# Products on quarter and half tiles of TensorE: an order tied product to product, and an order tied to its place only

## The chip, the cores and the metric

The kernel runs on one core of a Trainium2 chip. Its metric is the device time of one execution in microseconds (us); lower is better. Engines are named as in the profile: PE (TensorE matmul), PEld (its weight load), DVE (VectorE), ACT (ScalarE), POOL (GpSimd) and SP (SyncE, which issues most of the loads).

## What is computed

The reference is a two-layer encoder on 256 tokens of width 1024. Each layer runs two token mixers side by side, a gated DeltaNet in both directions and a differential attention. The change touches one step of the DeltaNet: the inverse of a unit triangular matrix for every chunk, head and direction, cut here to its lines.

```python
L = jnp.where(strict, jnp.einsum('bhncd,bhnmd->bhncm', kb, k) * decay, 0.0)
T = lax.linalg.triangular_solve(eye + L, jnp.broadcast_to(eye, L.shape),
                                left_side=True, lower=True, unit_diagonal=True)
u = jnp.einsum('bhncm,bhnme->bhnce', T, vb)
```

The kernel works with chunks of 128 tokens, two per sequence. There are 8 heads, in two groups of four, and two directions, so 32 triangles of 128 x 128 in each layer.

## The kernel before, in words

A layer is a row of projections (weights streamed from HBM, 512 columns at a time) with the DeltaNet's and the attention's small work laid between them. A projection (`proj_tm`) takes each weight block as two parts, `hi` (a cast on ACT, line 308) and `lo` (raw minus hi on DVE, line 310), and makes three products of 128 x 512 on PE for every block and token half (lines 324 to 326). In this document such a product is called a wide one. The tiles are `pp_gb`, `pp_ga` and `pp_pb` for the two merge gates and the attention's output projection.

The triangles are inverted in steps. 32 x 32 diagonal blocks are inverted by substitution on DVE. `merges(g)`, for head group g, then joins pairs of them to 64 x 64: it makes `y64p` (line 926), copies it on ACT, and makes the products `zt64` (line 939, 32 of them) and `z64` (line 944, 16 of them), each of 32 x 32. Each of these products lives on one of the sixteen 32 x 32 places of the PE array, given by the partitions it reads and those it writes. ACT then writes them, negated, back into the triangle `U_` (line 951) and into `T64` (line 954). `join()` does the same from 64 to 128 for both groups at once, on the four 64 x 64 places: `y128p` and `zt128`, each 32 products made by `quarters` (line 967), with copies on ACT behind each (lines 974, 976 and 984). From then on `chunks(g)` uses the finished triangle: `y1p`, `sp`, `ks`, `y2p`, `qs`, `po`, full products of 128 x 128 (lines 998 and 1037). `gram`, called by `weigh_q`, makes the products `kq` (line 789), also 128 x 128 and for four heads at a time, whose result DVE multiplies into `B` (line 830). A product in full f32 leaves two records in the trace.

The order is made by a scheduler when the kernel is built; each engine then runs its list strictly in that order, waiting by semaphores. `behind(x)` forbids the scheduler to issue what stands under it before instruction x has been issued; it adds no wait. `run(gen, at)` sets `mark["pin"]` to a certain wide product, the place of a step, and gives the step a high priority. Before the change, the first product of `zt64` is behind the pin, and each further one is behind the product before it; `quarters` chains its products in the same way.

On the other engines, this stretch also has: DVE's gating of the attention output (`ob`, line 1203), its transposition (`zb`, line 249) for a trip through DRAM issued by POOL, and its split (`ybT`, lines 263 and 265); DVE's `ktm` scaling (line 1010); and `key_sums`, which transposes `kq` on DVE (`tb_q`, line 135), squares it on ACT (line 1052), sums it on DVE into `qss` (line 1053), sends that through DRAM, and reduces it on DVE to `ssq` (line 1059).

Of the kernel before, what the change touches and what calls it, by code (L numbers as in the profile page):

```python
# [49 lines left out]
def hybrid_encoder(  # L50
# [19 lines left out]
    V, S, G, T = nc.vector, nc.scalar, nc.gpsimd, nc.tensor  # L70
# [24 lines left out]
    def bank_c(name):  # L95
        return ps_c.tile([P, 512], F32, tag="c", name=name)
# [7 lines left out]
    mark = {}  # L104
# [23 lines left out]
    blk = lambda b: slice(32 * b, 32 * b + 32)  # L128
# [141 lines left out]
    def behind(ins):  # L270
        return nullcontext() if ins is None else tc.issue_after(ins)
# [122 lines left out]
    halves = (slice(0, 64), slice(64, P))  # L394
# [6 lines left out]
    def srcdst(d, mm):  # L401
        return (2 * mm, 2 * mm + 1) if d == 0 else (2 * mm + 1, 2 * mm)
# [6 lines left out]
    for _ in range(5):  # L409
        mm = T.matmul(idle[:, :P], ones, ones, start=True, stop=True)  # L410
# [23 lines left out]
    for m in range(NM):  # L434
        mm = T.matmul(pos_p[:, m : m + 1], pos_r[:, m * P : (m + 1) * P], ones[0:1, 0:1], start=True, stop=True)
# [71 lines left out]
    for l in range(DEPTH):  # L507
# [120 lines left out]
        for kt in range(KT):  # L628
            for part in range(2):
                T.matmul(abp[0:64, :SEQ], wabr[:, kt, :], hT[kt // 4][:, part, kt % 4, :],  # L630
                         start=kt == 0 and part == 0, stop=kt == KT - 1 and part == 1)
# [3 lines left out]
        for m in range(NM):  # L635
            T.matmul(abq[:, m * 32 : (m + 1) * 32], abT[:, m * P : (m + 1) * P], id2,
                     start=True, stop=True)
# [244 lines left out]
        tix = lambda d, c, j4: (2 * d + c) * 4 + j4  # L882
        flat = lambda ap: ap.rearrange("p b e -> p (b e)")
        every = [(c, j4) for c in range(NM) for j4 in range(4)]
# [14 lines left out]
        def merges(g):  # L899

            U = U_[:, g]
            T64 = work.tile([P, 16, 64], F32, tag="w4c", name=f"T64{l}{g}", bufs=4)
            parts[g] = U, T64
            G.memset(T64[blk(0), 0:8, 32:64], 0.0)
            G.memset(T64[blk(3), 8:16, 0:32], 0.0)
            for b in range(4):
                co = 32 * (b % 2)
                (nc.sync if g else G).dma_start(out=T64[blk(b), :, co : co + 32],
                                                in_=udr[1, b, g].rearrange("t j i -> j t i"))
            yield  # L910
            for b in range(4 if g == 0 else 0):
                G.dma_start(out=U_[blk(b), :, :, blk(b)].rearrange("j g t i -> j (g t) i"),
                                  in_=udr[0, b].rearrange("g t j i -> j (g t) i"))
            yield
            v4 = lambda ap: ap.rearrange("p (c h i) -> p c h i", c=NM, h=4)
            y64p = v4(bank_c(f"y64p{l}{g}")[:, :256])
            y64 = work.tile([P, NM, 4, 32], F32, tag="w2c", name=f"y64{l}{g}", bufs=3)

            order = [(c, j4, mm, d) for c, j4 in every for mm in range(2) for d in range(2)]
            order.sort(key=lambda k: k != (0, 0, 1, 1))  # L920
            first = mark["pin"]
            for n_, (c, j4, mm, d) in enumerate(order):
                b0, b1 = srcdst(d, mm)
                co = 32 * (b0 % 2)
                with behind(first):
                    mm_ = T.matmul(y64p[blk(b1), c, j4, :], A[blk(b0), g, c, j4, blk(b1)],
                                   T64[blk(b0), tix(d, c, j4), co : co + 32], start=True, stop=True)
                if n_ == 0:
                    first = mm_.ins
            S.copy(y64, y64p)  # L930
            yield
            first = mark["pin"]
            zt64 = v4(bank_c(f"zt64{l}{g}")[:, :256])
            z64 = v4(bank_c(f"z64{l}{g}")[:, :256])
            for c, j4 in every:
                for mm, d in ((0, 0), (1, 1), (1, 0), (0, 1)):
                    b0, b1 = srcdst(d, mm)
                    with behind(first):
                        first = T.matmul(zt64[blk(b0), c, j4, :], y64[blk(b1), c, j4, :],
                                         U[blk(b1), tix(d, c, j4), blk(b1)], start=True, stop=True).ins  # L940
                for d in range(2):
                    b0, b1 = srcdst(d, d)
                    with behind(first):
                        first = T.matmul(z64[blk(b1), c, j4, :], U[blk(b1), tix(d, c, j4), blk(b1)],
                                         y64[blk(b1), c, j4, :], start=True, stop=True).ins
            for d in range(2):
                td = slice(8 * d, 8 * d + 8)
                fl = lambda z, b: z[blk(b)].rearrange("p c h i -> p (c h) i")
                for mm in range(2):
                    b0, b1 = srcdst(d, mm)  # L950
                    S.mul(U[blk(b0), td, blk(b1)], fl(zt64, b0), -1.0)
                b0, b1 = srcdst(d, d)
                co = 32 * (b0 % 2)
                S.mul(T64[blk(b1), td, co : co + 32], fl(z64, b1), -1.0)
            yield

        def join():

            v4 = lambda ap: ap.rearrange("p (c h i) -> p c h i", c=NM, h=4)
            every4 = [(c, j4, g, d) for c, j4 in every for g in range(2) for d in range(2)]  # L960

            def quarters(ps, lhs, rhs, row):
                last_ = mark["pin"]
                for c, j4, g, d in every4:
                    rows = halves[row(d)]
                    with behind(last_):
                        last_ = T.matmul(ps[g][halves[1 - row(d) if g == 0 else row(d)], c, j4, :],
                                         lhs(g, d, c, j4), rhs(g, d, c, j4), start=True, stop=True).ins

            y128p = [v4(bank_c(f"y128p{l}{g}")) for g in range(2)]  # L970
            y128 = [work.tile([P, NM, 4, 64], F32, tag="w2c", name=f"y128{l}{g}", bufs=3) for g in range(2)]
            quarters(y128p, lambda g, d, c, j4: A[halves[d], g, c, j4, halves[1 - d]],
                     lambda g, d, c, j4: parts[g][1][halves[d], tix(d, c, j4), :], lambda d: d)
            S.copy(y128[0], y128p[0])
            for d in range(2):
                S.copy(y128[1][halves[1 - d]], y128p[1][halves[d]])
            yield
            zt128 = [v4(bank_c(f"zt128{l}{g}")) for g in range(2)]
            quarters(zt128, lambda g, d, c, j4: y128[g][halves[1 - d], c, j4, :],
                     lambda g, d, c, j4: parts[g][0][halves[1 - d], tix(d, c, j4), halves[1 - d]], lambda d: 1 - d)  # L980
            for g in range(2):
                for d in range(2):
                    ha, hb = halves[d], halves[1 - d]
                    S.mul(parts[g][0][ha, 8 * d : 8 * d + 8, hb],
                          zt128[g][hb if g else ha].rearrange("p c h i -> p (c h) i"), -1.0)
            yield
# [204 lines left out]
        with tc.high_priority(offset=HP):  # L1191
            spread_blocks()
        mg = [merges(0), merges(1)]
        step(mg)
        step(mg)
# [201 lines left out]
```

## Time and profile before

| | |
|---|---|
| median of 3 runs | 749.97 us (749.54 to 751.45) |
| the profiled execution's own time | 749.41 us |
| its span (first to last instruction) | 747.6 us |
| granted clock of TensorE | 0.997 |
| PE busy | 738.6 us |
| DVE busy | 587.1 us |
| ACT busy | 482.5 us |
| POOL busy | 139.5 us |

In the timeline, a row has the start in us from the span's start, the time covered, the engine, the source line, the operation, what it writes and reads, and how many records were merged; at the end, in brackets, idle time ahead of it and what ended it. Since PE pipelines its products, its rows overlap, and the distance from one start to the next tells what a product costs. In the waits, a row has who waited for whom, the total, the number of times and the longest.

The region of the change lies at about 245 to 300 us in the first layer and 610 to 665 us in the second.

### The profile page before, as it was taken

How to read it: one execution, taken by the hardware profiler on the slowest of the kernel's cores; microseconds unless marked ns; L12 is line 12 of the kernel's file. 1: busy time of each engine (PE TensorE's matmuls, PEld its weight loads, DVE VectorE, ACT ScalarE, POOL GpSimd, SP SyncE). 2: the span in 40 equal slices, each digit the busy share in tenths (PEclk: the TensorE clock that was granted, in tenths of full speed). 3: DMA queues.
4: the chain of work that ended last, by engine and by line, in shares of the span. 5: the costliest groups of instructions: out<-in, count | busy, mean ns of one | idle time of the engine just before them, and what ended most of it. 6: DMA issues, size and time to landing. Idle time of an engine off the chain costs nothing.

```text
span 747.6 us, 13920 instructions
## 1 busy us (share of the span) xinstructions
PE 738.6 (99%) x5176; PEld 638.2 (85%) x5176; DVE 587.1 (79%) x1109; ACT 482.5 (65%) x1024; POOL 139.5 (19%) x221
## 2 busy tenths in 40 slices
PE   9999999999999999999999999999999999999996
PEld 6999889987888889988889899889778887988885
DVE  8696898999985975578677779999999679447782
ACT  6657875667876585645456578565687757766552
POOL 6004110112022422100000150202110424301000
PEclk9999999999999999999999999999999999999998
DMA  8755567776667462567674466767666747435641
GB/s 262 237 170 169 170 176 196 211 210 197 209 182 178 135 201 83 171 207 240 201 232 137 128 191 187 217 172 229 195 174 192 198 139 217 130 102 187 219 141 57
DMA packets 73734, 135.46 MB, mean 181 GB/s; under 512 B 12944, under 2 KB 13921, under 8 KB 73666
## 3 DMA queue, kind: packets, MB, share of 16 engines
q1 hardware_dynamic: 64750, 113.65, 50.8%
q0 software_dynamic: 7936, 19.35, 8.9%
q10 hardware_dynamic: 980, 1.58, 0.6%
q8 instruction: 41, 0.67, 0.4%
q14 instruction: 27, 0.22, 0.1%
HBM read 125.53 MB, written 9.01 MB: 180 GB/s over the span
## 4 chain that ended last, share of the span: by engine, by line
PE 90%; DVE 3%; issue 2%; ACT 2%; DMA 2%; POOL 1%; POOLq 0%; DVEq 0%; ACTq 0%
PE pp_vb L369 4%; PE pp_qk L325 4%; PE pp_qk L326 3%; PE pp_qk L324 3%; PE sc L1073 2%; PE pp_o L369 2%; PE pf_k L385 2%; PE pp_za L325 2%; PE pf_v L385 2%; PE pf_v L389 2%; PE pp_zb L324 2%; PE pf_q L387 2%; PE pf_k L387 2%; PE pf_k L389 2%; PE pf_q L385 2%
## 5 line engine op out<-in xcount | busy, mean ns | idle before, releaser
L325 PE MATMUL pp_qk<-lo_qk,hT 128*128 128x512 f32 x128 | 50.5, 395 | 0.3 <-DVE lo_qk L310 0.2
L326 PE MATMUL pp_qk<-hi_qk,hT 128*128 128x512 f32 x128 | 49.9, 390 | 0.0
L310 DVE TENSOR_TENSOR lo_qk<-raw_qk,hi_qk 128x1024 fp32r<-128x1024 f32 x32 | 39.1, 1221 | 10.3 <-ACT hi_qk L308 10.0
L324 PE MATMUL pp_qk<-hi_qk,hT 128*128 128x512 f32 x128 | 45.1, 393 | 0.0
L308 ACT CAST hi_qk<-raw_qk 128x1024 fp32r<-128x1024 f32 x28 | 29.4, 1049 | 23.5 <-PE pp_qk L326 12.4
L1083 ACT ACTIVATE es<-sc,mx 128x256 f32<-128x256 f32 x64 | 29.6, 474 | 19.5 <-DVE mx L1081 19.5
L387 PE MATMUL pf_q<-hT,hi_q 128*128 128x256 f32 x128 | 36.1, 286 | 0.0
L385 PE MATMUL pf_k<-hT,hi_k 128*128 128x256 f32 x128 | 36.0, 287 | 0.0
L385 PE MATMUL pf_v<-hT,hi_v 128*128 128x256 f32 x128 | 35.8, 285 | 0.0
L387 PE MATMUL pf_v<-hT,hi_v 128*128 128x256 f32 x128 | 35.8, 284 | 0.0
L385 PE MATMUL pf_q<-hT,hi_q 128*128 128x256 f32 x128 | 35.7, 284 | 0.0
L387 PE MATMUL pf_k<-hT,hi_k 128*128 128x256 f32 x128 | 35.7, 283 | 0.0
L389 PE MATMUL pf_q<-hT,lo_q 128*128 128x256 f32 x128 | 35.2, 288 | 0.0
L389 PE MATMUL pf_v<-hT,lo_v 128*128 128x256 f32 x128 | 34.5, 287 | 0.0
L310 DVE TENSOR_TENSOR lo_pb<-raw_pb,hi_pb 128x1024 fp32r<-128x1024 f32 x16 | 19.5, 1221 | 18.9 <-ACT hi_pb L308 18.8
L389 PE MATMUL pf_k<-hT,lo_k 128*128 128x256 f32 x128 | 34.3, 283 | 0.0
L308 ACT CAST hi_pa<-raw_pa 128x1024 fp32r<-128x1024 f32 x16 | 16.8, 1052 | 22.3 <-PE pp_pa L326 16.1
L679 DVE SCALAR_TENSOR_TENSOR cvq<-pf_q,cw,cvq 128x254 f32<-128x254 f32 (+1 forms) x64 | 30.0, 479 | 0.9 <-ACT cvq L675 0.2
L679 DVE SCALAR_TENSOR_TENSOR cvk<-pf_k,cw,cvk 128x254 f32<-128x254 f32 (+1 forms) x64 | 29.0, 477 | 1.3 <-ACT cvk L675 0.6
L679 DVE SCALAR_TENSOR_TENSOR cvv<-pf_v,cw,cvv 128x254 f32<-128x254 f32 (+1 forms) x64 | 29.7, 475 | 0.1
L325 PEld LDWEIGHTS pp_qk<-lo_qk,hT 128*128 128x128 f32 x128 | 24.0, 188 | 6.7 <-DVE lo_qk L310 1.7
L310 DVE TENSOR_TENSOR lo_pa<-raw_pa,hi_pa 128x1024 fp32r<-128x1024 f32 x16 | 19.6, 1224 | 11.1 <-ACT hi_pa L308 11.1
(415 smaller groups left out, 2543.0 us busy)
## 6 DMA issues: line engine op xcount, KB each, us to landing
raw_qk<-in_w_in_dram SPq DMA_DIRECT2D x32, 512.0 KB, 3.8
raw_k<-in_w_in_dram SPq DMA_DIRECT2D x16, 512.0 KB, 4.5
raw_q<-in_w_in_dram SPq DMA_DIRECT2D x16, 512.0 KB, 3.7
raw_v<-in_w_in_dram SPq DMA_DIRECT2D x16, 512.0 KB, 3.9
raw_zb<-in_w_in_dram SPq DMA_DIRECT2D x16, 512.0 KB, 3.8
raw_za<-in_w_in_dram SPq DMA_DIRECT2D x16, 512.0 KB, 3.8
raw_ga<-in_w_in_dram SPq DMA_DIRECT2D x16, 512.0 KB, 4.6
raw_pb<-in_w_pb_dram SPq DMA_DIRECT2D x16, 512.0 KB, 3.9
```

The costliest lines, as they stand in the source:

```text
L308: high = (V.tensor_copy if kp in turned else S.copy)(hi[:, :, :n], raw[:, :, :n]).ins
L310: mark[nm, kp] = high, V.tensor_tensor(lo[:, :, :n], raw[:, :, :n], hi[:, :, :n].bitcast(F32), ALU.subtract).ins
L324: T.matmul(o, act[kt // 4][:, 0, kt % 4, ts_], hi, start=kt == 0, stop=False)
L325: T.matmul(o, act[kt // 4][:, 0, kt % 4, ts_], lo, start=False, stop=False)
L326: mark["proj"] = T.matmul(o, act[kt // 4][:, 1, kt % 4, ts_], hi, start=False, stop=kt == KT - 1).ins
L369: mark["proj"] = T.matmul(o, act[kt // 4][:, pa, kt % 4, ts_], ws[kt][1 + pw], start=kt == 0 and n_ == 0, stop=kt == KT - 1 and n_ == 2).ins
L385: T.matmul(o, hi[:, cs], act[kt // 4][:, 0, kt % 4, :], start=first, stop=False, skip_group_check=True)
L387: T.matmul(o, hi[:, cs], act[kt // 4][:, 1, kt % 4, :], start=False, stop=False, skip_group_check=True)
L389: T.matmul(o, lo[:, cs], act[kt // 4][:, 0, kt % 4, :], start=False, stop=done, skip_group_check=True)
L679: V.scalar_tensor_tensor(ca[:, o0:o1], acc[:, b, o0 + sft : o1 + sft], cw[:, j, cb : cb + 1], ca[:, o0:o1], ALU.mult, ALU.add)
L1073: mm = T.matmul(sp[n][:, qt * SEQ : (qt + 1) * SEQ], qkT[h // 4][rows, 0, h % 4, qt * P : (qt + 1) * P], qkT[h // 4][rows, 1, h % 4, :], s ...
L1083: S.activation(es[:, n, qt, :], spv[:, qt, :], AF.Exp, bias=mx[:, n, qt : qt + 1], accum_out=s_all[:, h, n, qt : qt + 1])
```

## The change

Three things change in the source. In `merges`, all 32 products of `zt64` now come first and the 16 of `z64` after them, where before four of the one and two of the other alternated. The products of `zt64` are each behind the step's pin only, no longer behind one another, and those of `z64` have no tie. In `quarters`, each product is behind the pin only. No operation is added or removed, and no tile, buffer or semaphore is written by hand.

```diff
             for c, j4 in every:
-                for mm, d in ((0, 0), (1, 1), (1, 0), (0, 1)):
-                    b0, b1 = srcdst(d, mm)
-                    with behind(first):
-                        first = T.matmul(zt64[blk(b0), c, j4, :], y64[blk(b1), c, j4, :],
-                                         U[blk(b1), tix(d, c, j4), blk(b1)], start=True, stop=True).ins
+                for mm in range(2):
+                    for d in range(2):
+                        b0, b1 = srcdst(d, mm)
+                        with behind(first):
+                            T.matmul(zt64[blk(b0), c, j4, :], y64[blk(b1), c, j4, :],
+                                     U[blk(b1), tix(d, c, j4), blk(b1)], start=True, stop=True)
+            for c, j4 in every:
                 for d in range(2):
                     b0, b1 = srcdst(d, d)
-                    with behind(first):
-                        first = T.matmul(z64[blk(b1), c, j4, :], U[blk(b1), tix(d, c, j4), blk(b1)],
-                                         y64[blk(b1), c, j4, :], start=True, stop=True).ins
+                    T.matmul(z64[blk(b1), c, j4, :], U[blk(b1), tix(d, c, j4), blk(b1)],
+                             y64[blk(b1), c, j4, :], start=True, stop=True)
...
             def quarters(ps, lhs, rhs, row):
-                last_ = mark["pin"]
                 for c, j4, g, d in every4:
-                    rows = halves[row(d)]
-                    with behind(last_):
-                        last_ = T.matmul(ps[g][halves[1 - row(d) if g == 0 else row(d)], c, j4, :],
-                                         lhs(g, d, c, j4), rhs(g, d, c, j4), start=True, stop=True).ins
+                    with behind(mark["pin"]):
+                        T.matmul(ps[g][halves[1 - row(d) if g == 0 else row(d)], c, j4, :],
+                                         lhs(g, d, c, j4), rhs(g, d, c, j4), start=True, stop=True)
```

The scheduler then makes another order. It is shown at three places of layer 0; layer 1 has the same moves. The numbers in the names tell tiles apart: `zt_3358` and `z_3359` are `zt64` and `z64` of head group 1, `zt_3453` and `zt_3454` are `zt128` of groups 0 and 1, and `B_371<-kq_2855` is DVE's use of the last `kq`.

PE where the gate `pp_gb` ends and `pp_ga` begins, before:

```order
L789 MATMUL kq_2855<-kq_359 128x128
L939 MATMUL zt_3358<-U__96,y_3268 32x32
L789 MATMUL kq_2855<-kq_359 128x128
L939 MATMUL zt_3358<-U__96,y_3268 32x32
L789 MATMUL kq_2855<-kq_359 128x128
L939 MATMUL zt_3358<-U__96,y_3268 32x32
L789 MATMUL kq_2855<-kq_359 128x128
L939 MATMUL zt_3358<-U__96,y_3268 32x32
L944 MATMUL z_3359<-y_3268,U__96 32x32 x2
```

The same place now:

```order
L940 MATMUL zt_3358<-U__96,y_3268 32x32 x32
L945 MATMUL z_3359<-y_3268,U__96 32x32 x16
L325 MATMUL pp_gb_2765<-lo_gb_2820,hT_1_127 128x512
L326 MATMUL pp_gb_2765<-hi_gb_2819,hT_1_127 128x512
L324 MATMUL pp_gb_2766<-hi_gb_2819,hT_1_127 128x512
L325 MATMUL pp_gb_2766<-lo_gb_2820,hT_1_127 128x512
L326 MATMUL pp_gb_2766<-hi_gb_2819,hT_1_127 128x512
L789 MATMUL kq_2855<-kq_359 128x128 x4
```

The 48 small products of group 1 are in one piece, five wide products ahead of `kq`, and no `kq` product stands among them.

PE at `zt128`, in the gate `pp_ga`, before:

```order
L967 MATMUL zt_3453<-U__96,y_3416 64x64 x2
L324 MATMUL pp_ga_2897<-hi_ga_2952,hT_1_127 128x512
L325 MATMUL pp_ga_2897<-lo_ga_2953,hT_1_127 128x512
L967 MATMUL zt_3454<-U__96,y_3417 64x64 x2
L967 MATMUL zt_3453<-U__96,y_3416 64x64 x2
```

The same place now:

```order
L326 MATMUL pp_ga_2897<-hi_ga_2916,hT_0_126 128x512
L966 MATMUL zt_3453<-U__96,y_3416 64x64 x8
L966 MATMUL zt_3454<-U__96,y_3417 64x64 x8
L966 MATMUL zt_3453<-U__96,y_3416 64x64 x2
L966 MATMUL zt_3454<-U__96,y_3417 64x64 x2
```

The 32 products of `zt128` are in one piece, and stand about one and a half weight blocks earlier in the gate than before (ahead of `hi_ga_2934`, not within `hi_ga_2952`).

DVE in the same stretch, from the gating of the first token half on, before:

```order
L1203 SCALAR_TENSOR_TENSOR ob_1_384<-ob_1_384,rb_2865,zb_1_386 128x128 x4
L310 TENSOR_TENSOR lo_ga_2917<-raw_ga_2918,hi_ga_2916 128x1024
L1010 TENSOR_TENSOR ktm_360<-ktm_360,kds_372 128x512
L830 TENSOR_TENSOR B_371<-kq_2855,B_371 128x1024
L1010 TENSOR_TENSOR ktm_360<-ktm_360,kds_372 128x512
L1203 SCALAR_TENSOR_TENSOR ob_1_384<-ob_1_384,rb_2865,zb_1_386 128x128 x4
L249 STREAM_TRANSPOSE zb_1_386<-ob_1_384 128x4x4x32
L310 TENSOR_TENSOR lo_ga_2935<-raw_ga_2936,hi_ga_2934 128x1024
```

The same place now:

```order
L1202 SCALAR_TENSOR_TENSOR ob_1_384<-ob_1_384,rb_2865,zb_1_386 128x128 x4
L249 STREAM_TRANSPOSE zb_1_386<-ob_1_384 128x4x4x32
L830 TENSOR_TENSOR B_371<-kq_2855,B_371 128x1024
L310 TENSOR_TENSOR lo_ga_2917<-raw_ga_2918,hi_ga_2916 128x1024
L1009 TENSOR_TENSOR ktm_360<-ktm_360,kds_372 128x512 x2
L1202 SCALAR_TENSOR_TENSOR ob_1_384<-ob_1_384,rb_2865,zb_1_386 128x128 x4
L135 STREAM_TRANSPOSE tb_q_3491<-kq_359 128x512
L249 STREAM_TRANSPOSE zb_1_386<-ob_1_384 128x4x4x32
L310 TENSOR_TENSOR lo_ga_2935<-raw_ga_2936,hi_ga_2934 128x1024
```

Two transpositions (`tb_q_3491` and the second `zb_1`) now stand ahead of `lo_ga_2935`, and `B` ahead of `lo_ga_2917`.

## Prediction

> **What bounds the kernel now.** I read the page's shares of busy time first, then the waits of PE, then PE's timeline around the changed products.
>
> ```profile
> PE 738.6 (99%) x5176; PEld 638.2 (85%) x5176; DVE 587.1 (79%) x1109; ACT 482.5 (65%) x1024; POOL 139.5 (19%) x221
> ```
>
> PE is busy for 99% of the span. That alone doesn't say that it works at its peak, so the waits come next. In the two changed stretches, PE waits once:
>
> ```profile
> PE qs L998 <- DVE vtm L1018: 0.5, 1, 0.5
> ```
>
> This is layer 1's `qs`, waiting for DVE's subtraction. Everywhere else there PE runs its list without a gap, so what shortens the list ends the kernel sooner, and a new wait of PE lengthens it. What a group of products costs is read from starts. First group 0's small products standing alone between wide ones, and a `kq` group standing alone:
>
> ```profile
> 245.26 0.40 PE L326 MATMUL pp_gb<-hi_gb,hT 128*128 128x512 f32 x1
> 245.59 0.23 PE L939 MATMUL zt<-U__96,y 32*32 32x32 f32 x4
> ...
> 246.88 0.40 PE L325 MATMUL pp_gb<-lo_gb,hT 128*128 128x512 f32 x1
> 247.12 0.40 PE L326 MATMUL pp_gb<-hi_gb,hT 128*128 128x512 f32 x1
> 247.35 1.05 PE L789 MATMUL kq<-kq 128*128 128x128 f32 x8
> 248.16 0.48 PE L324 MATMUL pp_gb<-hi_gb,hT 128*128 128x512 f32 x1
> 248.48 0.40 PE L325 MATMUL pp_gb<-lo_gb,hT 128*128 128x512 f32 x1
> ```
>
> A wide product takes 0.23 us from start to start (247.12 to 247.35). From 245.26 to 246.88 PE does two wide products and the 48 small ones: 1.62 - 2 x 0.23 = 1.16 us for the small ones with both changes of shape. From 247.12 to 248.48 it does two wide ones and the `kq` group: 1.36 - 0.46 = 0.90 us. Now group 1's small products mixed with a `kq` group:
>
> ```profile
> 252.11 0.39 PE L326 MATMUL pp_gb<-hi_gb,hT 128*128 128x512 f32 x1
> 252.34 0.38 PE L789 MATMUL kq<-kq 128*128 128x128 f32 x2
> 252.65 0.24 PE L939 MATMUL zt<-U__96,y 32*32 32x32 f32 x2
> ...
> 255.33 0.50 PE L324 MATMUL pp_ga<-hi_ga,hT 128*128 128x512 f32 x1
> 255.66 0.39 PE L325 MATMUL pp_ga<-lo_ga,hT 128*128 128x512 f32 x1
> ```
>
> From 252.11 to 255.66 PE does two wide products, the same `kq` group and the same 48: 3.55 - 0.46 = 3.09 us, against 1.16 + 0.90 = 2.06 apart. Four times PE goes from a full product to a single small one, and three times back, and that costs 1.03 us. Layer 1 has the same, 2.98 us against 2.99 from the first `kq` to the next wide product:
>
> ```profile
> 617.48 0.38 PE L789 MATMUL kq<-kq 128*128 128x128 f32 x2
> ...
> 620.46 0.50 PE L324 MATMUL pp_ga<-hi_ga,hT 128*128 128x512 f32 x1
> ```
>
> The step from 64 to 128 shows `y128p` in one piece, and the equally large `zt128` cut in two:
>
> ```profile
> 260.68 0.39 PE L326 MATMUL pp_ga<-hi_ga,hT 128*128 128x512 f32 x1
> 261.00 1.16 PE L967 MATMUL y128p<-T,A 64*64 64x64 f32 x64
> 262.09 0.50 PE L324 MATMUL pp_ga<-hi_ga,hT 128*128 128x512 f32 x1
> 262.43 0.39 PE L325 MATMUL pp_ga<-lo_ga,hT 128*128 128x512 f32 x1
> ```
>
> ```profile
> 266.76 0.39 PE L326 MATMUL pp_ga<-hi_ga,hT 128*128 128x512 f32 x1
> 267.08 0.33 PE L967 MATMUL zt<-U__96,y 64*64 64x64 f32 x4
> ...
> 268.00 1.15 PE L967 MATMUL zt<-U__96,y 64*64 64x64 f32 x60
> ...
> 269.42 0.39 PE L324 MATMUL pp_ga<-hi_ga,hT 128*128 128x512 f32 x1
> ```
>
> One piece: 1.75 - 0.46 = 1.29 us. Two pieces, with four wide products: 2.66 - 0.92 = 1.74 us. The cut costs 0.45 us.
>
> **The change part by part.** *Group 1's small products in one piece, ahead of `kq`.* They lose the mixing: -1.03 us per layer, -2.06 in all. *`zt128` in one piece:* -0.45 per layer, -0.90 in all.
>
> *The products of `zt64` first, those of `z64` after them.* The count stays; what can change is the rate. Before, six products on six different places of the array followed one another; now 32 run over four places, then 16 over two, those two in different rows of the array. The nearest row for a less varied order is `y64p`, in which each place gets two products in a row:
>
> ```profile
> 240.10 1.47 PE L926 MATMUL y64p<-T,A 32*32 32x32 f32 x128
> 241.49 0.50 PE L325 MATMUL pp_gb<-wgb,hT 128*128 128x512 f32 x1
> ```
>
> 128 records in 1.39 us are 10.9 ns each. The 96 records of a group's `zt64` and `z64` take 1.16 us with the changes of shape, or 0.71 without them, if the two changes cost what the cut of `zt128` does, 0.45: 7.4 to 12.1 ns each. I take no change. The worse end is `z64`'s 32 records at 3.5 ns more, 0.11 us in each of the four groups, +0.45 in all; the better end is a sixth of a group's 1.16, 0.2 each, -0.8 in all, as four places used evenly might gain.
>
> *The wait of 0.5 us* in layer 1's `qs` belongs to DVE's subtraction. In that layer DVE stood behind `rq`, which waits for POOL; the new order puts two of the four subtractions ahead of `rq`. I take -0.5, and 0 as the other end.
>
> *More pieces.* The program has 134 runs of wide products behind narrower full ones, against 128, so some five more changes of this kind. The price is at most the 0.09 us by which 248.16 to 248.48 exceeds a wide product: +0.45; the `kq` group's 0.90 for a block whose own starts cover 0.81 contains one such change already, and says that a block's last record is cheaper by as much. I take +0.1.
>
> *The waits behind the pieces.* What follows a piece needs ACT to have copied it, with these times of one copy:
>
> ```profile
> L951 ACT ACTIVATE U__96<-zt x16: 360/376/380, 246.6 to 622.0; 32x256 f32<-32x256 f32 x16
> ```
>
> Six copies of 0.38 take 2.3 us. Between the small products of group 1 and `y128p` stand now 14 wide products and the `kq` group, 14 x 0.23 + 0.90 = 4.1 us: covered, with 1.8 to spare. If the cover were gone, the 2.3 us would be paid in each layer.
>
> *DVE's new order* is the tight place. DVE has no idle time there and does two transpositions more ahead of `lo_ga_2935`:
>
> ```profile
> 258.83 1.09 DVE L249 STREAM_TRANSPOSE zb<-ob 128x512 f32<-128x512 f32 x1
> 259.78 1.20 DVE L310 TENSOR_TENSOR lo_ga<-raw_ga,hi_ga 128x1024 fp32r<-128x1024 f32 x1
> ...
> 265.01 0.70 DVE L135 STREAM_TRANSPOSE tb_q<-kq 128x512 f32<-128x512 f32 x1
> ```
>
> It began at 259.78; now it begins about 0.95 + 0.70 = 1.65 later, at 261.4, and ends at 262.6. PE needs it in the second wide product after `zt128`. PE gets there so: the small piece starts behind the wide product at 250.98 (five of 0.23 ahead of 252.11); 250.98 + 0.23 + 1.16 + 5 x 0.23 + 0.90 + 9 x 0.23 + 1.29 + 14 x 0.23 + 1.29 + 0.23 = 262.4. So PE waits 0.1 to 0.2 us in each layer: +0.3. The ends are 0, and 0.95 per layer if the longer transposition counts in full behind an exact meeting.
>
> *The trip of `qss` through DRAM.* DVE's `ssq` waits for it, and behind `ssq` stand a `lo_ga` and the subtractions that `y2p` and `qs` need:
>
> ```profile
> 275.88 0.68 DVE L1053 TENSOR_REDUCE qss<-tb_q 128x16 f32<-128x512 f32 x1
> ...
> 286.05 0.27 DVE L1059 TENSOR_REDUCE ssq<-qss 128x16 f32<-128x64 f32 x1 [3.03 <-DMA qss<-qdr]
> ```
>
> The trip takes 286.05 - 276.56 = 9.5 us. Counting DVE's list in the same manner, the last sum now ends near 271.3, `ssq` comes at 280.8, and the last subtraction ends at 287.7, where PE's second `qs` wants it at 288.1. The slack is 0.4 us; I take +0.05 per layer for it, +0.1.
>
> The sum: -2.06 - 0.90 - 0.5 + 0.1 + 0.3 + 0.1 = -2.96 us, rounded to -3.0. The profiled execution's 749.41 us (span 747.6) would become 746.4. The runs' median of 749.97 lies 0.56 above that execution; I carry the difference over: 747.0 us.
>
> By the Trainium skill's page TensorEngine Tiling (Array Packing), section Restrictions and Gotchas, different row tiles cannot access the same PSUM bank simultaneously. This speaks against the new order, in which all of `zt64`, and then all of `z64`, goes to one bank; the rival on banks below works it out from rows. No row here separates the banks from the places.
>
> **The rivals.** *One bank at a time.* If products into one bank follow one another and only those into another bank overlap, then before, the 32 of `zt64` set the pace of a group and the 16 of `z64` lay beside them: up to 1.16 / 32 = 0.036 us each. After, `z64` pays 16 x 0.036 = 0.58 on its own, four times: +2.3, and the sum is -0.7, 749.3 us. For it: half of `z64`'s neighbours changed. Against it: `y64p` changes banks at each product and is no faster for that, 10.9 ns a record.
>
> *A place takes one product per round.* If a round of products took its 0.145 us (1.16 / 8) whatever its size, the four groups would each have 16 rounds in place of 8, +4.6 us, and the sum would be +1.6: 751.6. `y64p`'s 43 ns for four records on one place speak against it.
>
> *PE gains what DVE and ACT then take back.* PE comes 1.5 us earlier in each layer to consumers whose suppliers haven't gained. If half is lost in waits for `lo_ga` or for copies, the sum is -1.5: 748.5. For it: the slacks of -0.1 and 0.4 us above. Against it: all others that I counted are over 0.8.
>
> *The trip through DRAM ends on the other side: slower.* The place is `ssq`, with the `lo_ga` and four subtractions queued behind it on DVE. Each us beyond a trip of 9.9 us is a us of PE's in each layer. At (3.0 + 2.25) / 2 = 2.6 us beyond, or 12.5 us, the kernel is slower by 0.3%; at 13 us, 749.97 - 3.0 + 6.2 = 753.2. For it: DVE idled 3.03 us for the trip already before. Against it: that idling shows how late it came with PE still unharmed, and its four small loads and one store only meet other weights' loads, as before.
>
> *That the change does nothing* is excluded by the order on PE, which is fixed when the kernel is built.
>
> **How the numbers follow.** Some 0.3%, 2.25 us, is what a measurement of this kernel can tell from no change, so faster means under 747.7. The forecast has 0.62; PE's gain taken back 0.19; one bank at a time 0.08; one product per round 0.04; the slow trip 0.07. The first gives faster, with a share of 0.02 added from the second, whose smaller losses still end under 747.7: 0.64. No change has the rest of the second, the banks, and half of the rounds: 0.27. Slower has the trip and the other half: 0.09. The low end of the range is the forecast with the better packing and no wait at all, 747.0 - 0.8 - 0.4, with a little for the median: 745.6. The high end takes in PE's gain taken back and the banks: 749.6. Beyond it lie the rounds and the trip, 0.11.
>
> **What would show it.** In the profile after, the small products of group 1 should take 1.16 us with their changes, `kq` 0.90 on its own, `zt128` 1.29 in one row of 64 records, and no `kq` row should lie among `zt` rows. A group's 96 records over 1.3 us would show the packing lost. The waits of PE should show a `pp_ga` waiting for `lo_ga` for some tenths, and no `qs` for more. A PE wait of over 1 us for DVE behind `ssq`, or for an ACT copy, would make the prediction wrong, and so would PE waits of over 0.8 us in all in each layer.

## The result and the profile after

| | before | after |
|---|---|---|
| median of 7 runs each | 749.79 us (749.08 to 751.45) | 746.91 us (746.65 to 748.52) |
| ratio, with its 95% interval | | 0.9963 (0.9952 to 0.9975) |
| span of the profiled execution | 747.6 us | 745.2 us |
| PE busy | 738.6 us | 736.4 us |

The kernel is 0.37% faster, and the median lies 0.09 us under the prediction. The span of the profiled execution became 2.4 us shorter, not 3.0, and its terms are not those of the prediction. First the whole list of what PE waited for in after:

```profile
PE idle L410 <- DVE ones L407: 1.1, 1, 1.1
PE pp_vb L464 <- ACT wktm_vb L308: 0.3, 1, 0.3
PE pp_vb L464 <- ACT hT L234: 0.2, 1, 0.2
PE pp_qk L325 <- DVE lo_qk L310: 0.2, 1, 0.2
```

None lies in the two changed stretches: three stand at the start of the program, and the last one stands between the stretches, at 446 us. The wait of `qs` for DVE is gone, and the wait of a `pp_ga` for `lo_ga`, which the prediction expected for 0.1 to 0.2 us in each layer, did not come. Next PE's timeline of layer 0 at the two head groups and at the `kq` that was mixed with the second:

```profile
245.26 0.40 PE L326 MATMUL pp_gb<-hi_gb,hT 128*128 128x512 f32 x1
245.59 0.72 PE L940 MATMUL zt<-U__96,y 32*32 32x32 f32 x62
...
246.17 0.65 PE L945 MATMUL z<-y,U__96 32*32 32x32 f32 x30
...
247.08 0.40 PE L325 MATMUL pp_gb<-lo_gb,hT 128*128 128x512 f32 x1
...
251.18 0.39 PE L324 MATMUL pp_gb<-hi_gb,hT 128*128 128x512 f32 x1
251.50 0.75 PE L940 MATMUL zt<-U__96,y 32*32 32x32 f32 x64
252.11 0.69 PE L945 MATMUL z<-y,U__96 32*32 32x32 f32 x32
252.73 0.50 PE L325 MATMUL pp_gb<-lo_gb,hT 128*128 128x512 f32 x1
253.07 0.40 PE L326 MATMUL pp_gb<-hi_gb,hT 128*128 128x512 f32 x1
...
253.77 0.39 PE L326 MATMUL pp_gb<-hi_gb,hT 128*128 128x512 f32 x1
254.00 1.05 PE L789 MATMUL kq<-kq 128*128 128x128 f32 x8
...
255.12 0.40 PE L325 MATMUL pp_ga<-lo_ga,hT 128*128 128x512 f32 x1
```

Read as before, with two wide products of 0.23 us taken off: group 0's piece takes 1.82 - 0.46 = 1.36 us, where it took 1.16. Group 1's takes 1.89 - 0.46 = 1.43, and `kq` alone 1.35 - 0.46 = 0.89; together 2.32, against 3.09 when they were mixed. The 32 records of `z` cost as much as the 64 of `zt`: 0.62 us (252.11 to 252.73, with the change back to a wide product) against 0.61. Now `zt128`:

```profile
261.44 0.39 PE L326 MATMUL pp_ga<-hi_ga,hT 128*128 128x512 f32 x1
261.76 1.44 PE L966 MATMUL zt<-U__96,y 64*64 64x64 f32 x64
263.13 0.50 PE L324 MATMUL pp_ga<-hi_ga,hT 128*128 128x512 f32 x1
263.46 0.39 PE L325 MATMUL pp_ga<-lo_ga,hT 128*128 128x512 f32 x1
```

It is in one piece, but takes 2.02 - 0.46 = 1.56 us. The prediction had 1.29, and the two pieces of before took 1.74. On DVE, the split that was the tight place, and the two ends of the trip of `qss`:

```profile
261.60 1.22 DVE L310 TENSOR_TENSOR lo_ga<-raw_ga,hi_ga 128x1024 fp32r<-128x1024 f32 x1
...
270.66 0.67 DVE L1052 TENSOR_REDUCE qss<-tb_q 128x16 f32<-128x512 f32 x1
...
279.68 0.26 DVE L1058 TENSOR_REDUCE ssq<-qss 128x16 f32<-128x64 f32 x1 [4.36 <-DMA qss<-qdr]
```

`lo_ga` ends at 262.82, 0.2 us later than forecast. PE comes to it only at 263.46, 1.06 us later than forecast; 0.74 of that is due to the pieces ahead of it, which are 0.20, 0.27 and 0.27 us longer than forecast. The trip takes 279.68 - 271.33 = 8.35 us.

### The profile page after: what moved, and what is told of

It reads as the page before. It is cut to its first block, busy times and chain, and to the rows that moved or that the text cites. A ratio compares the mean times of both kernels' runs of the same rounds, so it can differ in the third digit from the quotient of the medians.

```text
span 745.2 us, 13923 instructions
## 1 busy us (share of the span) xinstructions
PE 736.4 (99%) x5176; PEld 638.4 (86%) x5176; DVE 585.9 (79%) x1109; ACT 482.5 (65%) x1024; POOL 141.8 (19%) x221
## 4 chain that ended last, share of the span: by engine, by line
PE 96%; ACT 2%; issue 1%; DVE 1%; POOLq 0%; POOL 0%; DVEq 0%; ACTq 0%
PE pp_vb L369 4%; PE pp_qk L325 4%; PE pp_qk L326 3%; PE pp_qk L324 3%; PE sc L1072 2%; PE pp_o L369 2%; PE pf_k L385 2%; PE pp_za L325 2%; PE pf_v L385 2%; PE pf_v L389 2%; PE pp_gb L325 2%; PE pp_gb L324 2%; PE pp_zb L324 2%; PE pf_q L387 2%; PE pf_k L387 2%; PE pf_v L387 2%
```

## The experiments

Each kernel is a version of before, unless after is named, with the edit shown. The time it is set against is that of before on the same chip.

**Only the merges.** `merges` as in after, `quarters` with the ties of before. Against after, that is:

```diff
+                last_ = mark["pin"]
                 for c, j4, g, d in every4:
+                    rows = halves[row(d)]
-                    with behind(mark["pin"]):
-                        T.matmul(ps[g][halves[1 - row(d) if g == 0 else row(d)], c, j4, :],
-                                         lhs(g, d, c, j4), rhs(g, d, c, j4), start=True, stop=True)
+                    with behind(last_):
+                        last_ = T.matmul(ps[g][halves[1 - row(d) if g == 0 else row(d)], c, j4, :],
+                                         lhs(g, d, c, j4), rhs(g, d, c, j4), start=True, stop=True).ins
```

> The merges as in the change, the joins tied as before. Its PE list is that of the changed kernel but for the first 16 products of zt128, which go round all four 64 x 64 places and not eight times over two. Theory, places: a place of the array takes one record after the other (about 58 ns for 64 columns), so zt128 costs 1.29 us like y128p, not 1.56 as in the changed kernel: 0.27 less in each layer, about 746.4 us where the changed kernel has 746.9; a wait of PE of 0.1 to 0.2 for lo_ga may come back. Rival, the gain comes from untying the joins: then this kernel loses a third of it and has 748 or more.

Measured: 746.43 us (745.93 to 748.04) against 749.54; ratio 0.9953 (0.9940 to 0.9965); span 744.6. PE's list differs from after's in the first 16 products of `zt128` alone. They go around the four places:

```profile
261.52 0.39 PE L326 MATMUL pp_ga<-hi_ga,hT 128*128 128x512 f32 x1
261.84 1.16 PE L968 MATMUL zt<-U__96,y 64*64 64x64 f32 x64
262.93 0.50 PE L324 MATMUL pp_ga<-hi_ga,hT 128*128 128x512 f32 x1
263.27 0.39 PE L325 MATMUL pp_ga<-lo_ga,hT 128*128 128x512 f32 x1
```

1.75 - 0.46 = 1.29 us, the value forecast for after. So the 0.27 us that after's `zt128` takes more come from its order, eight products on two places and then eight on the other two. `zt128` is in one piece although its ties stand: it is the edit in `merges` that brings that.

**Only the joins.** `merges` as before, `quarters` as in after. Against before, that is:

```diff
-                last_ = mark["pin"]
                 for c, j4, g, d in every4:
-                    rows = halves[row(d)]
-                    with behind(last_):
-                        last_ = T.matmul(ps[g][halves[1 - row(d) if g == 0 else row(d)], c, j4, :],
-                                         lhs(g, d, c, j4), rhs(g, d, c, j4), start=True, stop=True).ins
+                    with behind(mark["pin"]):
+                        T.matmul(ps[g][halves[1 - row(d) if g == 0 else row(d)], c, j4, :],
+                                         lhs(g, d, c, j4), rhs(g, d, c, j4), start=True, stop=True)
```

> The joins as in the change, the merges as before (four of zt64, two of z64, tied). zt128 is then in one piece and nearly in turn over the four places, and zt64 of group 1 is still mixed with kq. Theory: the cut of zt128 is gone, 0.45 us in each layer, and nothing else: 0.9 less, about 748.9 us. Rival, the gain is in the joins: as fast as the changed kernel, 746.9. Rival, the gain is in the other engines' order and not in PE's pieces: no change, 749.8.

Measured: 749.1 us (748.61 to 749.61) against 749.54; ratio 0.9989 (0.9980 to 0.9998); span 747.0. The spans differ by 0.6 us and the medians by 0.44, where 0.9 was expected. `zt128` is in one piece, but late (it starts at 266.73, where after's starts at 261.76), and PE now waits for ACT's copy behind it:

```profile
PE y1p L996 <- ACT U__96 L982: 0.5, 2, 0.3
```

Group 1 stays mixed with `kq` here. The joins' part of the change is worth at most 0.2% by itself, and beside the merges it costs 0.27 us in each layer.

**Before, with ACT's copies in another order.** All ties and all products of before; ACT writes the four copies into `U_` ahead of the two into `T64`.

```diff
+            fl = lambda z, b: z[blk(b)].rearrange("p c h i -> p (c h) i")
             for d in range(2):
                 td = slice(8 * d, 8 * d + 8)
-                fl = lambda z, b: z[blk(b)].rearrange("p c h i -> p (c h) i")
                 for mm in range(2):
                     b0, b1 = srcdst(d, mm)
                     S.mul(U[blk(b0), td, blk(b1)], fl(zt64, b0), -1.0)
+            for d in range(2):
+                td = slice(8 * d, 8 * d + 8)
                 b0, b1 = srcdst(d, d)
                 co = 32 * (b0 % 2)
                 S.mul(T64[blk(b1), td, co : co + 32], fl(z64, b1), -1.0)
```

> The kernel before, all ties and the order of the products kept; only ACT's copies in merges are written in another order, the four of zt64 first and the two of z64 behind them. Built so, group 1's small products stand in one piece ahead of kq, with the places still mixed. Theory: group 1 loses the mixing, 1.03 us in each layer, and keeps the better packing (1.16 for 48 products, not 1.36), so -2.1, and -0.5 more if the wait of qs goes as well: 747.2 to 747.7 us. Rival, it is the missing ties that help: no change, 749.8. Rival, the slow z64 products of the changed kernel come from standing in one piece and not from their order: group blocks of 1.36, 748.5 us.

Measured: 748.81 us (747.75 to 750.81) against 749.54; ratio 0.999 (0.998 to 1.000); span 746.1. This gained less than expected. Group 1's 48 products do stand in one piece ahead of `kq`, with the ties in place:

```profile
251.63 0.39 PE L324 MATMUL pp_gb<-hi_gb,hT 128*128 128x512 f32 x1
...
252.90 0.50 PE L325 MATMUL pp_gb<-lo_gb,hT 128*128 128x512 f32 x1
253.23 0.40 PE L326 MATMUL pp_gb<-hi_gb,hT 128*128 128x512 f32 x1
```

They take 1.60 - 0.46 = 1.14 us, so neither the loss of the ties nor the grouping by product is needed for that. But PE gives part of it back, since `y1p` waits for the copies behind a `zt128` that is still cut in two:

```profile
269.12 1.05 PE L1000 MATMUL y1p<-vtm,U__96 128*128 128x128 f32 x7 [0.59 <-ACT U__96 L986]
```

It waits as long in layer 1, 1.2 us in all, and that is what the expectation lacked. In starts, the wide product ahead of `y1p` takes 0.98 us (268.14 to 269.12) in place of 0.23, so the two waits cost some 1.5 us. The profiled execution, at 747.83, is the second fastest of the twelve; why the median lies 1 us above it, no run shows.

**Two places at a time, in two rows of the array.** The group's products in three turns, each on two places, and each product behind the one before it; the first two turns alternate `zt` and `z`, so their results go to two banks, and the third has two places of `zt`, in one bank. `quarters` is as in after.

```diff
...
+            for two in (((0, 0), (1,)), ((1, 1), (0,)), ((0, 1), (1, 0))):
+                for c, j4 in every:
+                    for of in two:
+                        first = zt_(c, j4, *of) if len(of) == 2 else z_(c, j4, *of)
...
```

> The changed kernel with the 48 small products of a group in another order: two places at a time, in two different rows of the array, and (in two thirds of them) in two different PSUM banks: zt64 and z64 in turn, then zt64 over two places. The cost of a group's piece between wide products was 1.16 us before and 1.36 in the changed kernel. Theory, places: a place takes a record in about 31 ns, so two places give a record in 15.7 and 96 records take 1.51, with the change of shape 1.9 us. Rival, banks: alternating banks run at the full rate of 8.3 ns a record, only the last third at 15.7: 1.4 us. Rival, rows: as places here, 1.9 us.

**Two places at a time, in one row.** The same with the `z` of the first two turns exchanged, so that the two places of a turn share a row.

```diff
-            for two in (((0, 0), (1,)), ((1, 1), (0,)), ((0, 1), (1, 0))):
+            for two in (((0, 0), (0,)), ((1, 1), (1,)), ((0, 1), (1, 0))):
```

> The same, but the two places of the first two thirds lie in the same row of the array (they read the same partitions), and their banks differ. Theory, places: the same as with two rows, 1.9 us for a group's piece. Rival, rows: a row takes one record in 31 ns, so 64 x 31 + 32 x 15.7 ns = 2.5, with the change of shape 2.85 us. Rival, banks: 1.4 us.

Measured: 748.45 us and 748.92, one run each, against 749.95; spans 746.7 and 747.2. The timeline of PE at group 0, first with two rows:

```profile
244.75 0.39 PE L326 MATMUL pp_gb<-hi_gb,hT 128*128 128x512 f32 x1
...
245.15 0.19 PE L938 MATMUL zt<-U__96,y 32*32 32x32 f32 x1
...
245.46 0.19 PE L938 MATMUL zt<-U__96,y 32*32 32x32 f32 x1
...
246.85 0.40 PE L325 MATMUL pp_gb<-lo_gb,hT 128*128 128x512 f32 x1
```

And with one row:

```profile
245.15 0.40 PE L326 MATMUL pp_gb<-hi_gb,hT 128*128 128x512 f32 x1
...
245.56 0.19 PE L938 MATMUL zt<-U__96,y 32*32 32x32 f32 x1
...
245.88 0.19 PE L938 MATMUL zt<-U__96,y 32*32 32x32 f32 x1
...
247.26 0.40 PE L325 MATMUL pp_gb<-lo_gb,hT 128*128 128x512 f32 x1
```

From 245.15 to 245.46, and from 245.56 to 245.88, a record of `zt` follows another ten times, with one of `z` beside each: 31 to 32 ns from one to the next on the same place. In the third turns, which go to one bank, single records of a place are 32 ns apart too, as are those of after's `z` (two places in two rows, one bank). So neither the row nor the bank sets the pace, but the place: it takes a record of a 32 x 32 product about every 32 ns. The column of the array (the places that write the same partitions) doesn't set it either. In before, two of a group's six places lie in one column, and a steady round gives each place two records:

```profile
246.22 0.23 PE L939 MATMUL zt<-U__96,y 32*32 32x32 f32 x4
...
246.32 0.23 PE L939 MATMUL zt<-U__96,y 32*32 32x32 f32 x4
```

That round has 12 records in 0.10 us, and four of them go to that one column: 25 ns each, less than the 32 of a place.

The whole groups take 2.10 - 0.46 = 1.64 and 2.11 - 0.46 = 1.65 us, between the 1.9 of the theory of places and the 1.4 of that of banks, so neither sum came out; it is the single starts that tell the two apart. With two rows, the three turns begin at 245.06, 245.48 and 245.89, 0.41 us apart, though the 16 records of a place take 0.51: the next turn's first products begin on their free places while the last ones of the turn before still wait for theirs, which the 1.9 did not allow for.

The Trainium skill's page TensorEngine Tiling (Array Packing), section Restrictions and Gotchas, says that different row tiles cannot access the same PSUM bank simultaneously. These rows show no price of that: two places in two rows are as fast with one bank (after's `z`, 32 ns) as with two (here, 31 to 32 ns).

**All pieces, and products that go around the places.** The order of before within a group (four `zt`, two `z`), without ties; ACT's copies in the order of the third experiment; the products of `z64` lose their ties in the same way as those of `zt64` below; in `quarters` the two products that need ACT's last copies stand first, and the others go around the four places behind them without further ties.

```diff
-                        first = T.matmul(zt64[blk(b0), c, j4, :], y64[blk(b1), c, j4, :],
-                                         U[blk(b1), tix(d, c, j4), blk(b1)], start=True, stop=True).ins
+                        T.matmul(zt64[blk(b0), c, j4, :], y64[blk(b1), c, j4, :],
+                                 U[blk(b1), tix(d, c, j4), blk(b1)], start=True, stop=True)
...
-                for c, j4, g, d in every4:
-                    rows = halves[row(d)]
+                for n_, (c, j4, g, d) in enumerate([(c, j4, g, d) for c, j4 in every for g in (1, 0) for d in (1, 0)]):
                     with behind(last_):
-                        last_ = T.matmul(ps[g][halves[1 - row(d) if g == 0 else row(d)], c, j4, :],
-                                         lhs(g, d, c, j4), rhs(g, d, c, j4), start=True, stop=True).ins
+                        mm_ = T.matmul(ps[g][halves[1 - row(d) if g == 0 else row(d)], c, j4, :],
+                                       lhs(g, d, c, j4), rhs(g, d, c, j4), start=True, stop=True)
+                    if n_ < 2:
+                        last_ = mm_.ins
```

> Every step in one piece and in turn over as many places as it has: the products of merges in the order of before (four of zt64, two of z64) without ties to each other, ACT's four copies of zt64 ahead of the two of z64, and in quarters the two products that need the last copies first, all others behind them. Theory: against the changed kernel 0.20 less for each of the four groups and 0.27 less for zt128 in each layer, -1.3 us, 745.6; waits of PE for lo_ga of up to 0.2 in each layer may take some of it back. Rival, PE is no longer what bounds there: as the changed kernel, 746.9.

Measured: 745.38 us (744.74 to 747.25) against 749.95; ratio 0.9943 (0.9928 to 0.9957); span 743.1. Group 0, and `zt128`:

```profile
245.01 0.39 PE L326 MATMUL pp_gb<-hi_gb,hT 128*128 128x512 f32 x1
...
246.62 0.40 PE L325 MATMUL pp_gb<-lo_gb,hT 128*128 128x512 f32 x1
...
263.41 0.39 PE L326 MATMUL pp_ga<-hi_ga,hT 128*128 128x512 f32 x1
263.73 1.16 PE L968 MATMUL zt<-U__96,y 64*64 64x64 f32 x64
...
265.16 0.39 PE L325 MATMUL pp_ga<-lo_ga,hT 128*128 128x512 f32 x1
```

1.61 - 0.46 = 1.15 us for the group and 1.75 - 0.46 = 1.29 for `zt128`: this has the pieces of after with the rate of before, and no wait of PE in the two stretches.

**The same for `y64p`.** In addition, group 1's products of `y64p` start at another place than group 0's, so that the same place isn't used twice in a row. All engines' lists are otherwise those of the last kernel.

```diff
-            order = [(c, j4, mm, d) for c, j4 in every for mm in range(2) for d in range(2)]
+            order = [(c, j4, mm, d) for c, j4 in every for mm in ((1, 0) if g else (0, 1)) for d in range(2)]
```

> The same, and y64p of head group 1 goes round the places half a turn off group 0's, so that no place gets two products in a row. Theory, places: 128 records at 8.3 ns and not 10.9, 0.3 less in each layer, 0.6 us less than without it: 745.0. Rival, y64p's pace is set by its waits for the loads of T64 or by what PE is fed, not by places: no difference, 745.6.

Measured: 746.19 us (746.05 to 748.24) against 749.95; ratio 0.9955 (0.9941 to 0.9969); span 745.8. A miss, 1.2 us over the expectation. `y64p` itself became 0.12 us shorter in each layer, where 0.3 was expected. And PE waited, in layer 1 for `lo_ga` and in layer 0 for `vtm`:

```profile
PE pp_ga L325 <- DVE lo_ga L310: 1.4, 1, 1.4
...
PE qs L1001 <- DVE vtm L1021: 0.3, 1, 0.3
```

What came late to DVE were two trips through DRAM. These are ACT's `ybT` of layer 1, which DVE's `ybT` and then `lo_ga` stand behind, and DVE's `ssq` of layer 0:

```profile
629.45 1.21 ACT L263 ACTIVATE ybT<-zb,nw 128x512 fp32r<-128x512 f32 x1 [1.97 <-DMA zb<-bny_yb]
```

```profile
271.85 0.69 DVE L1056 TENSOR_REDUCE qss<-tb_q 128x16 f32<-128x512 f32 x1 [0.42 <-ACT tb_q L1055]
282.00 0.26 DVE L1062 TENSOR_REDUCE ssq<-qss 128x16 f32<-128x64 f32 x1 [3.52 <-DMA qss<-qdr]
```

The trip of `qss` took 282.00 - 272.54 = 9.46 us. The question was whether the new order of `y64p` did that or the execution, so three more kernels ran on one chip: after with that one line, and both of the last two again.

> The kernel after, with the y64p products of head group 1 rotated by half a turn and nothing else changed; every engine's list is otherwise the same. Theory (the rotation speeds y64p by 0.12 us per layer and costs nothing; what made e7 slower in its profile were two trips through DRAM that happened to take longer): the span 0.2 us under that of after, time 746.4 to 746.9, y64p's 128 products 1.28 us in place of 1.39. Rival (the rotation has a price of its own of about 1 us): 747.7 or more.

> The same kernel as e6, for its scatter beside e10 on one chip. Theory (the trips of zb and of qss through DRAM differ from run to run by up to 3 us, and PE waits when they take more than about 8.5): 745.4 again, runs from 744.7 to 747.3, and where the profile shows ssq more than 8.5 us behind the last sum of qss, PE waits for vtm in y2p or qs. Rival (e6 and e7 differ by themselves): 0.8 us under e10, with no such wait in either.

> The same kernel as e7. Its lists differ from those of e9 only in the place order within y64p. Theory (long trips by chance in e7): 745.2, the same as e9 within 0.4 us, and a profile whose PE waits go with the trips and not with y64p. Rival: 0.8 us above e9 again.

Measured, against 749.77: after with the one line 746.68 us (746.36 to 748.36), ratio 0.9964 (0.9951 to 0.9976), span 744.6; the kernel without the rotation again 745.62 (744.74 to 748.22), ratio 0.9950 (0.9934 to 0.9966), span 744.0; with it again 745.37 (744.86 to 748.33), ratio 0.9952 (0.9937 to 0.9966), span 743.4. The last two can't be told apart, and neither has a wait of PE in the stretches. The ends of the trip of `qss` in the last:

```profile
272.45 0.69 DVE L1056 TENSOR_REDUCE qss<-tb_q 128x16 f32<-128x512 f32 x1 [0.42 <-ACT tb_q L1055]
279.12 0.26 DVE L1062 TENSOR_REDUCE ssq<-qss 128x16 f32<-128x64 f32 x1
```

At most 279.12 - 273.14 = 5.98 us, where the same program had taken 9.46. So the rotation is not what made that execution slow. Its profile shows the two late trips, and PE's two waits behind them make 1.7 of the 2.4 us by which its span exceeds that of the repeat. Why a trip is long in one execution and short in another, no run shows. `y64p` in after with the rotation:

```profile
239.75 1.34 PE L926 MATMUL y64p<-T,A 32*32 32x32 f32 x128
241.03 0.50 PE L325 MATMUL pp_gb<-wgb,hT 128*128 128x512 f32 x1
```

It takes 1.28 us, where it took 1.39 in before and 1.40 in after (240.09 to 241.49): the 0.12 expected. That makes 0.2 us of 745, which the medians can't resolve.

## Why the prediction was right, and which of its steps were not

The time came out at the forecast, and its mechanism, fewer changes of shape on an engine that has no other slack, is what the runs show. But some terms failed and made up for one another. From the starts of PE's products in the two profiles, for both layers:

| term | forecast | measured |
|---|---|---|
| group 1 apart from `kq` | -2.06 | -2.06, less the packing below |
| packing of `zt64` and `z64` | 0 (-0.8 to +0.45) | +0.94 (0.20 and 0.27 in each layer) |
| `zt128` in one piece | -0.90 | -0.36 |
| `qs` in layer 1 | -0.5 | -0.84 |
| `lo_ga` | +0.3 | 0 |
| more pieces, trip of `qss` | +0.2 | -0.11 (the rest) |
| sum | -2.96 | -2.43 |

*The mixing* was right: with the rate of before, the third experiment has group 1's piece at 1.14 us, and `kq` alone takes 0.89 in after; 1.16 and 0.90 were forecast.

*"I take no change" for the rate of the small products* is the step that failed. The prediction took `y64p`'s 10.9 ns as the nearest row and bounded `z64`'s loss by 3.5 ns a record. `y64p` uses four places at a time. `z64` uses two, each place takes a record every 32 ns, and so its records come every 16 ns, where before's came about every 8.3 in their steady part. The worse bound, +0.45, was half of what was measured. All four groups take 1.36 or 1.43 us, over the 1.3 that the prediction had named as the sign of a lost packing. The rival on banks had a loss of the same kind for another cause, and the fourth and fifth experiments leave banks no part in it.

The rival that came nearest in kind is *a place takes one product per round*: a place does take its products one after another, but in 63 ns each (two records), not in 145. The argument against it misread a row: the 128 records of `y64p` lie on four places, so 43 ns (1.39 us / 32) is the time that a place had for one record, not for four.

*`zt128` at 1.29 us* failed for a reason of the same kind, the order within the piece. It is in one piece as forecast, but its first 16 products go eight by eight on two places; the first experiment has it at 1.29 with another order of these alone. The order printed in the change showed that sequence, and the prediction didn't price it.

*"So PE waits 0.1 to 0.2 us" for `lo_ga`* failed in the main as a consequence: DVE was on time within 0.2 us, and PE came 1.06 us later than forecast (263.46 in place of 262.4), 0.74 of it by the three pieces. The rest are two slips in the working: its terms add up to 262.5, and between group 1's small products and `y128p` the timeline has 15 wide products, not 14. With the pieces as forecast, PE would have come at 262.7, with `lo_ga` ready at 262.82: at most the lower end of the wait. With faster pieces no wait came either (the sixth experiment), but that kernel has another order on DVE, so it doesn't say what after's order would have done.

*`qs`*: the wait in layer 1 went as forecast, but it was priced by its idle time and not by starts, as everything else was. In before:

```profile
657.88 0.43 PE L998 MATMUL qs<-ktm,kq 128*128 128x128 f32 x2
658.85 1.83 PE L998 MATMUL qs<-ktm,kq 128*128 128x128 f32 x14 [0.55 <-DVE vtm L1018]
660.43 0.47 PE L326 MATMUL pp_ga<-hi_ga,hT 128*128 128x512 f32 x1
```

These 16 records take 2.55 us to the next wide product's start, and after's 16 take 1.71 (652.64 to 654.35): 0.84 us less, and not 0.5. That the 134 runs of wide products cost +0.1 did not show; what is left is -0.11 for both layers, and no experiment took it apart.

*The trip of `qss` through DRAM* was right for after: 8.35 us is inside the 9.9 allowed. The rival built on it was no idle one. In the seventh experiment, a trip of 9.46 us and a late `zb` cost PE waits, and a kernel whose median was 745.37 when it was run again took 747.56 in the profiled execution. Against before's 749.97 that is not slower.

The difference of the medians, 2.9 us, exceeds that of the two spans, 2.4. Both lie in the interval of the ratio, 1.9 to 3.6 us, so that the median hit the forecast to 0.1 us is partly luck.

## What to carry to other kernels

Small products of one shape belong in one piece, and within it they should go around at least four places of the array: a group of 48 cost 1.15 us around six places, 1.36 to 1.43 when four and then two were used, 1.64 when two were. The loss is that of the two: in after's group 1, the 64 records on four places took 0.61 us and the 32 on two places 0.62. When a change regroups products by what they compute, write out which place each one uses, and price the part with the fewest places by a row that has as few. And where a supplier stands behind a trip through DRAM, judge its slack by several executions: the same program showed 6 and 9.5 us.

## What the runs showed of the hardware

A place of 32 x 32 takes a record of a full f32 product every 32 ns, whether the other place at work lies in its row or not, and whether both write to one bank or to two. A group on six places takes 8.3 ns a record at its steady part; there a place gets a record only every 50 ns, so something other than the places sets that pace, and no run shows what. Products on 64 x 64 places behave alike: the 64 records of `zt128` take 1.09 us from their start to the next wide product's when they go around four places, and 1.37 when the first quarter goes to one pair of places and the second to the other pair. Each pair has a bank of its own there, so at this size the runs don't tell the place from the bank.
